# Attention maxima of a sparse-attention decoder step: edge masks as VectorE additions instead of bf16 matmuls, and a new table of durations in the kernel's planner

## The chip, the cores and the metric

The kernel runs on one core of a Trainium2 chip. Times are device microseconds of that core: the median of several runs, and, for everything that is read from a trace, one profiled execution. TensorE is called PE, VectorE DVE, ScalarE ACT, GpSimd POOL and SyncE SP, as in the profile.

## The reference, cut to what matters

One layer of a hybrid decoder: an adaptive norm, one input projection, native sparse attention beside a gated MLP, and an output projection, for a prompt of 1024 tokens and for 8 tokens that are decoded against caches. The change touches the prompt's attention, and there the maxima that keep the exponentials of two branches in range: `s` over the selected blocks, `w` over a sliding window of 512 keys.

```python
def block(i):
    start = i * Q_BLOCK
    qb = lax.dynamic_slice_in_dim(q, start, Q_BLOCK, axis=1)
    qpos = start + jnp.arange(Q_BLOCK, dtype=jnp.int32)
    kwb = lax.dynamic_slice_in_dim(kw_pad, start, band, axis=1)
    ...
s_s = jnp.einsum('bqgrd,bqgnld->bqgrnl', qg, k_sel).astype(jnp.float32) * scale
s_s = jnp.where(m_s, s_s, NEG).reshape(B, Tq, N_KV, GQA, n_sel * L_SLC)
p_s = jax.nn.softmax(s_s, axis=-1).reshape(B, Tq, N_KV, GQA, n_sel, L_SLC)
m_w = ((kwpos[None, :] <= qpos[:, None]) & (kwpos[None, :] > qpos[:, None] - WINDOW)
       & (kwpos[None, :] >= 0))[None, :, None, None, :]
s_w = jnp.einsum('bqgrd,bkgd->bqgrk', qg, kw).astype(jnp.float32) * scale
p_w = jax.nn.softmax(jnp.where(m_w, s_w, NEG), axis=-1)
```

## The kernel before, in words

The work runs in stages that overlap at their edges: loads, modulation and projections of the prompt (to about 260 us of the trace), the decoded tokens with their caches (to about 430 us), the prompt's attention (to about 807 us), the merge of the two mixers (to about 937 us) and the output projection. Large products are split into a high and a low fp32r half, so that three fp32r matmuls stand for one fp32 product.

Attention goes over 16 tiles, `TILES`: a key/value group `g` and a block `i` of 128 queries, four heads at a time. For each tile three streams of instructions are recorded:

- `front(g, i)` loads the queries, splits them into `R` and `R2`, computes the compressed branch (`kc`, `ce`, `pg`) and, by `peaks()` and `maxima()`, the row maxima of raw scores: `wm`, one for each 128 keys of the window, and `bm`, one for each 64-key block. From these, with the choice of blocks, it makes the biases `BT`, which PE transposes into `R2`.
- `scores()` computes 128 keys by 512 (four heads of 128 queries) into a bank of the tag `st`, two fp32r matmuls each; ACT takes the exponential `pt`, and POOL cuts the edge blocks with an affine select. `low()` splits `pt` into `p`'s high and low halves on ACT, DVE and POOL.
- `outputs()` multiplies `p` with the values `vv` into a bank `pv`, three matmuls for each of 132 groups; `weigh()` and `close()` apply sums and gates.

`maxima()` takes up to four 128-column blocks at a time: one matmul `mx<-L,R` for the adjacent blocks of a head, into one of two banks of the tag `mx`, then one DVE reduction. A block on the diagonal (`k == i`) needs a triangle mask, and the oldest of a window (`k == i - 4`) its complement, the far mask. They are added by PE, as a matmul of a bf16 identity with a bf16 mask, into the same bank. The two `mx` banks serve every transpose and small product of the stage too.

Beside attention PE works through gate pieces, `ct_proj` (24 fp32r matmuls of 344 columns, `mm<-hh,c0h` and the like), which depend on nothing in attention and are let in at a pace that `paced()` ties to the value groups done.

No order is written out by hand. While the program is recorded, the class `Plan` keeps an estimated time for each engine, tile and bank: `op()` looks up when operands are free, `cost()` gives a duration, and `go()` takes, among the streams that can go on, the one whose next operand is due first against PE's estimated time, and by rank after that. What `cost()` says thus decides in which order each engine's queue is written; on the chip each engine then follows its queue in order and waits where an operand is late. Every instruction is issued through one line of the class `Proxy`, L218 before the change and L235 after it, so rows are told apart by their tiles' names.

Of the kernel before, what the change touches and what calls it, by code (L numbers as in the profile page):

```python
# [28 lines left out]
class Pack:  # L29


    def __init__(self):
        self.cols, self.parts, self.n = {}, [], 0
# [57 lines left out]
MAIN, PACK1, PACKD, ROPE, EROWS = _tables()  # L91


class Plan:
# [6 lines left out]
    def __init__(self):  # L101
        self.free, self.bus, self.slots, self.rings, self.seen = {}, 0.0, {}, {}, {}
        self.columns, self.streams, self.last = {}, [], 0.0
        self.gone, self.since, self.spilled = 0.0, {}, {}

    def tile(self, pool, uid, shape, dtype, name, bufs=1):
        t = pool.tile(shape, dtype, name=name, tag=name, bufs=bufs)
        n = self.rings.get((uid, name), 0)
        self.rings[uid, name] = n + 1
        self.slots[t.tensor.name] = (uid, name, n % bufs)  # L110
        return t
# [54 lines left out]
    def cost(self, engine, name, outs, ins, size, start):  # L166
        if engine == "pe":
            n, m, dt = ins[1].free_size(), ins[0].free_size(), ins[0].dtype
            cost, passes = max(n / 2.4 + 2.5, (26 if dt == BF else 104) * m / 128), 1
            if name == "transpose":  # L170
                passes = 2
            elif dt == F32:
                cost, passes = max(4 * n / 2.4 / (4 if m <= 32 else 1), 208 * m / 128), 4
            tick = int(start // self.TICK)
            self.columns[tick] = self.columns.get(tick, 0.0) + passes * n * ins[0].partition_size() / 128
            return cost * (2 if self.cold(start) else 1)
        if engine == "dve":
            plain = name == "tensor_copy" and outs[0].space == ins[0].space
            return 67 + (0.52 if plain else 1.042) * size
        if engine == "act":  # L180
            return (280 if len(ins) > 1 else 70) + 0.834 * size
        if name == "affine_select":
            return 65 + 1.4 * size
        if name == "tensor_scalar":
            return max(330 + 0.83 * size, 3.61 * size - 28)
        return (300 + 165 * size if size < 16 else 70 + 2.27 * size)

    def op(self, engine, name, outs, ins):
        size = max(x.free_size() for x in outs + ins)
        start = self.free.get(engine, 0.0)  # L190
        for x in ins:
            start = max(start, self.after(x, True, engine))
        for x in outs:
            start = max(start, self.after(x, False, engine))
        for x in ins + outs:
            if x.space == PSUM:
                start = max([start] + [y[2] for y in self.seen.get(self.box(x)[0], ()) if y[3] != engine])
        if "dma" in name:
            self.free[engine] = start + (1038.0 if engine == "pool" else 450.0)
            self.bus = max(self.bus, self.free[engine]) + outs[0].free_nbytes() * outs[0].partition_size() / 359.0  # L200
            end = self.bus + 2000.0
        else:
            cost = self.cost(engine, name, outs, ins, size, start)
            self.free[engine] = start + cost
            end = start + cost + self.LATE[engine]
            self.last = max(self.last, end + 60.0)
        for x in ins:
            self.note(x, False, end, engine)
        for x in outs:
            self.note(x, True, end, engine)  # L210
# [50 lines left out]
def nsa_gmlp_step(ctx: ExitStack, tc: tile.TileContext, a: dict):  # L261
    nc = tc.nc
    plan = Plan()
    dve, act, pool, pe, sp = (plan.engine(e, n) for e, n in (
        (nc.vector, "dve"), (nc.scalar, "act"), (nc.gpsimd, "pool"), (nc.tensor, "pe"), (nc.sync, "sp")))
# [13 lines left out]
    def region(name, side):  # L279
        return Region(name, side)  # L280
# [4 lines left out]
    def bank(tag):  # L285
        return plan.tile(psum, "psum", [128, 512], F32, tag, 2)
# [12 lines left out]
    turn = [0]  # L299
# [5 lines left out]
    def dma(out, in_):  # L305
        sp.dma_start(out, in_)

    def rows(name, n, m=128):

        return bass.AP(tensor=a[name].tensor, offset=a[name].offset, ap=[[0, m], [1, n]])  # L310

    def consts(pack, tile_, name, p=128):
        lo, hi = pack.cols[name]
        return tile_[:p, lo:hi]


    const = region("const", "left")
    main = const.tile([128, MAIN.n], F32, name="main")

    def K(name, p=128):  # L320
        return consts(MAIN, main, name, p)

    ident = K("ident")
    ident_bf = const.tile([128, 128], BF, name="ident_bf")
    tri_bf = const.tile([128, 128], BF, name="tri_bf")
    far_bf = const.tile([128, 128], BF, name="far_bf")
    minus_half = const.tile([128, 16], F32, name="minus_half")
    gates = const.tile([128, NT + 1, 24], F32, name="gates")
    wck = const.tile([128, 2, 128], F32, name="wck")
# [232 lines left out]
    pk = rawreg.tile([128, PACK1.n], F32, name="pk")  # L562
# [8 lines left out]
    def rope_tab(which):  # L571

        c = top.tile([128, NT + 1, 2, 64], F32, name="rt")
        g = gq[:, which, None, :]
        for hf in range(2):
            lo, other = slice(hf * 32, hf * 32 + 32), slice(32 - hf * 32, 64 - hf * 32)
            n = [128, NT + 1, 32]
            pool.tensor_tensor(c[:, :, 0, lo], rope[:, :, 0, :], g[:, :, lo].to_broadcast(n), op=OP.mult)
            pool.tensor_tensor(c[:, :, 1, lo], rope[:, :, 1 + hf, :], g[:, :, other].to_broadcast(n), op=OP.mult)
        return c  # L580

    def constants():

        dma(rope, a["rope"])
        dma(gq.rearrange("p a b -> p (a b)"), rows("qk_g", 128))
        pool.memset(wck, 0.0)
        for j in range(2):
            for g in range(2):
                dma(wck[g * 64:g * 64 + 64, j, g * 64:g * 64 + 64], a["w_cmp"][j])
        yield lambda: stage[0] >= 3  # L590
        tabs["k"] = rope_tab(1)
        yield lambda: stage[0] >= 6
        dve.tensor_copy(ident_bf, ident)
        yield 0
        dve.tensor_copy(tri_bf, consts(PACK1, pk, "tri"))
        dve.tensor_copy(far_bf, consts(PACK1, pk, "far"))
        yield lambda: all(("k", i) in passed for i in ORDER)
        tabs["q"] = rope_tab(0)
        dma(pd, a["packd"])
        dma(pg_i, a["pages"])  # L600
        yield pg_i
        dve.tensor_copy(pg_f, pg_i)
        dve.tensor_scalar(idx, pg_f, 16.0, consts(PACKD, pd, "jmod"), op0=OP.mult, op1=OP.add)
# [905 lines left out]
    built, part = set(), set()  # L1509
# [63 lines left out]
    def front(g, i):  # L1573

        nb = 2 * (i + 1)
        j = TILES.index((g, i))
# [11 lines left out]
        b = bank("mx").rearrange("p (r q) -> p r q", r=4)  # L1588
# [12 lines left out]
        def maxima(w, flat, c, width, dst):  # L1601

            b = bank("mx")
            part = flat[c:c + 4]
            j = 0
            while j < len(part):
                r, k = part[j]
                n = sum(1 for x in part[j:] if x[0] == r)
                pe.matmul(b[:, j * 128:(j + n) * 128], lhsT=R[:, r, :], rhs=L1[g, w][:, k * 128:(k + n) * 128],
                          start=True, stop=False, skip_group_check=True)  # L1610
                for x in range(n):
                    mask = tri_bf if k + x == i else far_bf if w and k + x == i - 4 else None
                    if mask is not None:
                        pe.matmul(b[:, (j + x) * 128:(j + x + 1) * 128], lhsT=ident_bf, rhs=mask,
                                  start=False, stop=False, skip_group_check=True)
                j += n
            n = len(part) * 128
            dve.tensor_reduce(dst[:, c * 128 // width:(c * 128 + n) // width],
                              b[:, :n].rearrange("p (a x) -> p a x", x=width), op=OP.max, axis=AX.X)
# [16 lines left out]
        b = bank("mx")[:, :256].rearrange("p (r c) -> p r c", r=4)  # L1636
# [13 lines left out]
        if i == 0:  # L1650
# [5 lines left out]
                           op=OP.mult)  # L1656
# [14 lines left out]
        b = bank("mx")  # L1671
# [19 lines left out]
        b = bank("mx")  # L1691
# [326 lines left out]
```

## Time and profile before

| what | value |
|---|---|
| median of 3 runs | 1044.58 us (1043.27 to 1046.47) |
| the profiled execution, its own time | 1043.74 us |
| its span, first to last instruction | 1041.8 us |
| mean granted TensorE clock | 0.995 |
| PE busy | 1015.5 us, 5763 matmuls |
| DVE busy | 632.8 us |
| ACT busy | 448.4 us |
| POOL busy | 305.2 us |

Matmuls are pipelined, and a matmul's shown duration overlaps the next one's. What one costs is seen from the distance between starts. The same holds, less strongly, for DVE.

### The profile page before, as it was taken

How to read it: one execution, taken by the hardware profiler on the slowest of the kernel's cores; microseconds unless marked ns; L12 is line 12 of the kernel's file. 1: busy time of each engine (PE TensorE's matmuls, PEld its weight loads, DVE VectorE, ACT ScalarE, POOL GpSimd, SP SyncE). 2: the span in 40 equal slices, each digit the busy share in tenths (PEclk: the TensorE clock that was granted, in tenths of full speed). 3: DMA queues.
4: the chain of work that ended last, by engine and by line, in shares of the span. 5: the costliest groups of instructions: out<-in, count | busy, mean ns of one | idle time of the engine just before them, and what ended most of it. 6: DMA issues, size and time to landing. Idle time of an engine off the chain costs nothing.

```text
span 1041.8 us, 16312 instructions
## 1 busy us (share of the span) xinstructions
PE 1015.5 (97%) x5763; PEld 878.7 (84%) x5763; DVE 632.8 (61%) x1340; ACT 448.4 (43%) x951; POOL 305.2 (29%) x332
## 2 busy tenths in 40 slices
PE   6899999999999999999999999999999999999998
PEld 2489887879999999987787787788788999998776
DVE  1673686454668766568679868885753247574322
ACT  2762122001322254766776676676666242232000
POOL 0442475454321110013444332433333100251000
PEclk8999999999999999999999999999999999999999
DMA  8836441104775745422121121111111478654321
GB/s 294 292 95 211 155 131 51 61 21 152 271 213 162 245 154 184 141 68 60 51 56 56 47 68 50 45 51 57 50 57 58 138 238 259 182 161 137 129 90 64
DMA packets 106312, 130.35 MB, mean 125 GB/s; under 512 B 27299, under 2 KB 71525, under 8 KB 106230
## 3 DMA queue, kind: packets, MB, share of 16 engines
q1 hardware_dynamic: 101622, 112.53, 34.4%
q0 software_dynamic: 4608, 16.78, 5.2%
q8 instruction: 45, 0.74, 0.3%
q14 instruction: 37, 0.30, 0.1%
HBM read 98.96 MB, written 30.23 MB: 124 GB/s over the span
## 4 chain that ended last, share of the span: by engine, by line
PE 81%; DVE 7%; ACT 4%; DMA 3%; issue 2%; POOL 1%; SPq 1%; DVEq 0%; ACTq 0%; POOLq 0%
PE mm L218 33%; PE pv L218 20%; PE st L218 15%; PE mx L218 14%; DVE p L218 2%; DMA graw<-in_w_ada_dram 1%; DVE ce L218 1%; DVE bm L218 1%; ACT p L218 1%; ACT pt L218 1%; DVE wm L218 1%; SPq L218 1%; DVE c0l L218 0%; DVE hl L218 0%; POOL m L218 0%
## 5 line engine op out<-in xcount | busy, mean ns | idle before, releaser
L218 PE MATMUL pv<-p,vv 128*128 128x512 f32 (+1 forms) x396 | 112.2, 402 | 0.1
L218 PE MATMUL mm<-hh,c0h 128*128 128x344 f32 x320 | 105.1, 328 | 0.0
L218 PE MATMUL mm<-hh,c1h 128*128 128x344 f32 x320 | 104.9, 328 | 0.0
L218 ACT ACTIVATE pt<-st 128x512 f32<-128x512 f32 x132 | 78.6, 595 | 55.7 <-PE st L218 53.7
L218 PE MATMUL mm<-hl,c0h 128*128 128x344 f32 x320 | 102.2, 319 | 0.0
L218 PE MATMUL mm<-hh,c1l 128*128 128x344 f32 x320 | 102.2, 319 | 0.0
L218 PE MATMUL mm<-hh,c0l 128*128 128x344 f32 x320 | 102.1, 319 | 0.0
L218 PE MATMUL mm<-hl,c1h 128*128 128x344 f32 x320 | 102.1, 319 | 0.0
L218 PE MATMUL st<-R,L 128*128 128x512 f32 (+1 forms) x264 | 88.8, 418 | 0.0
L218 PEld LDWEIGHTS pv<-p,vv 128*128 128x128 f32 (+1 forms) x396 | 65.8, 173 | 21.9 <-DVE p L218 1.4
L218 DVE TENSOR_TENSOR p<-pt,p 128x512 fp32r<-128x512 f32 x88 | 70.3, 807 | 13.0 <-ACT p L218 12.5
L218 POOL TENSOR_TENSOR p<-pt,p 128x512 fp32r<-128x512 f32 x44 | 59.1, 1344 | 43.9 <-ACT p L218 43.9
L218 ACT ACTIVATE p<-pt 128x512 fp32r<-128x512 f32 x94 | 59.1, 629 | 16.6 <-POOL pt L218 14.4
L218 PE MATMUL mx<-L,R 128*128 128x512 f32 (+3 forms) x204 | 63.1, 362 | 1.2 <-DVE bm L218 0.6
L218 PEld LDWEIGHTS mm<-hh,c0h 128*128 128x128 f32 x320 | 60.4, 189 | 2.8 <-issue 0.2
L218 POOL TENSOR_SCALAR_AFFINE_SELECT pt<-pt 128x512 f32<-128x512 f32 x40 | 27.8, 696 | 119.0 <-ACT pt L218 117.1
L218 PEld LDWEIGHTS mm<-hh,c1h 128*128 128x128 f32 x320 | 60.3, 188 | 2.4 <-issue 0.2
L218 PEld LDWEIGHTS mm<-hh,c0l 128*128 128x128 f32 x320 | 60.2, 188 | 2.2
L218 PEld LDWEIGHTS mm<-hh,c1l 128*128 128x128 f32 x320 | 60.2, 188 | 2.2
L218 PEld LDWEIGHTS mm<-hl,c1h 128*128 128x128 f32 x320 | 60.1, 188 | 0.0
L218 PEld LDWEIGHTS mm<-hl,c0h 128*128 128x128 f32 x320 | 60.1, 188 | 0.0
L218 ACT ACTIVATE th<-mm 128x344 f32<-128x344 f32 x68 | 30.9, 454 | 58.3 <-PE mm L218 58.0
(495 smaller groups left out, 2622.1 us busy)
## 6 DMA issues: line engine op xcount, KB each, us to landing
t_db<-th SPq DMA_DIRECT2D x24, 172.0 KB
t_da<-th SPq DMA_DIRECT2D x24, 172.0 KB
th<-t_db SPq DMA_DIRECT2D x24, 172.0 KB
th<-t_da SPq DMA_DIRECT2D x24, 172.0 KB
graw<-in_w_ada_dram SPq DMA_DIRECT2D x16, 256.0 KB
araw<-in_w_ada_dram SPq DMA_DIRECT2D x16, 256.0 KB
xt<-in_x_dram SPq DMA_DIRECT2D x8, 512.0 KB
eraw<-in_w_ada_dram SPq DMA_DIRECT2D x16, 256.0 KB
```

The costliest lines, as they stand in the source:

```text
L218: r = getattr(real, name)(*args, **kw)
```

## The change

Two parts. In `maxima()` the mask matmuls go, and after the score matmuls of a bank DVE adds the fp32 mask in place in PSUM, one instruction for all blocks of the bank that need the same mask; the masks are kept in fp32 and the bf16 identity goes. In `Plan`, `cost()` and `op()` get other numbers: fp32r matmuls cost 0.4375 ns a column and 7 ns instead of 1/2.4 and 2.5; a price (`turn`) is put on changes between three kinds of matmul (split fp32r, full arrays in fp32, bf16 or transposes, and partial fp32); reciprocals and ACT instructions from SBUF or on few partitions cost more; and transfers take longer, above all those in rows under 512 bytes.

```diff
+            form, passes, turn = "split", 1, 0.0
+            if dt == FR and name != "transpose":
+                cost = max(0.4375 * n + 7.0, 104 * m / 128)
+                turn = {"split": 0.0, "full": 85.0, "part": 190.0}[self.form]
...
-            self.bus = max(self.bus, self.free[engine]) + outs[0].free_nbytes() * outs[0].partition_size() / 359.0
-            end = self.bus + 2000.0
+            self.bus = max(self.bus, self.free[engine]) + outs[0].free_nbytes() * outs[0].partition_size() / (179.5 if short else 359.0)
+            end = self.bus + (4200.0 if short else 2200.0)
...
-    ident_bf = const.tile([128, 128], BF, name="ident_bf")
-    tri_bf = const.tile([128, 128], BF, name="tri_bf")
-    far_bf = const.tile([128, 128], BF, name="far_bf")
+    tri = const.tile([128, 128], F32, name="tri")
+    far = const.tile([128, 128], F32, name="far")
...
-                for x in range(n):
-                    mask = tri_bf if k + x == i else far_bf if w and k + x == i - 4 else None
-                    if mask is not None:
-                        pe.matmul(b[:, (j + x) * 128:(j + x + 1) * 128], lhsT=ident_bf, rhs=mask,
-                                  start=False, stop=False, skip_group_check=True)
                 j += n
+            for mask, edge in ((tri, i), (far, i - 4 if w else -1)):
+                at = [j for j, (_, k) in enumerate(part) if k == edge]
+                if at:
+                    step = at[1] - at[0] if len(at) > 1 else 1
+                    x = b.rearrange("p (a x) -> p a x", x=128)[:, at[0]:at[-1] + 1:step, :]
+                    dve.tensor_tensor(x, x, mask[:, None, :].to_broadcast([128, len(at), 128]), op=OP.add)
```

What the two parts do to the order is seen at three places. The first is PE's queue amid the maxima of one tile (`R_5931` before and `R_5928` after belong to it; `L_4323` and `L_4261` are its keys, `vv` the values, `mm` a gate piece). Before:

```order
L218 MATMUL mx<-L_4323,R 128x512
L218 LDWEIGHTS ident_bf
L218 MATMUL mx<-tri_bf,ident_bf 128x128
L218 MATMUL mx<-L_4323,R 128x512
L218 MATMUL st<-R,L_4324 128x512
L218 MATMUL st<-R_5931,L_4327 128x512
L218 MATMUL pv<-p_6391,vv_4330 128x512
```

After, from the same matmul of the maxima on:

```order
L235 MATMUL mx<-L_4261,R 128x512
L235 MATMUL mx<-main,s_6388 128x128 x4
L235 MATMUL st<-R,L_4262 128x512
L235 MATMUL st<-R_5928,L_4265 128x512
L235 MATMUL pv<-p_6485,vv_4268 128x512
L235 MATMUL pv<-p_6485,vv_4268 64x512
L235 MATMUL pv<-p_6485,vv_4268 128x512
L235 MATMUL mm<-hh,c0h 128x344
```

The identity's load and the mask are gone from PE, the next maxima come later, and a gate piece stands between them.

The second is DVE's queue at that place (`bm` and `wm` are the maxima, `p` the split of the probabilities). Before:

```order
L218 TENSOR_TENSOR p_6366<-pt,p_6366 128x512
L218 TENSOR_REDUCE wm<-mx 128x4
L218 CAST p_6421<-pt 128x512
L218 TENSOR_REDUCE bm<-mx 128x8
L218 TENSOR_TENSOR p_6421<-pt,p_6421 128x512
L218 TENSOR_REDUCE bm<-mx 128x8 x2
```

After:

```order
L235 TENSOR_TENSOR mx<-mx,tri 128x128
L235 TENSOR_REDUCE bm<-mx 128x8
L235 TENSOR_TENSOR p_6511<-pt,p_6511 128x512
L235 TENSOR_REDUCE bm<-mx 128x8
L235 TENSOR_TENSOR mx<-mx,tri 128x128
L235 TENSOR_REDUCE bm<-mx 128x8 x2
L235 CAST p_6571<-pt 128x512
```

Each reduction of a bank with an edge block now has an addition ahead of it, in the queue from which PE also gets the low halves `p`.

The third is PE's queue near the start (`graw` and `araw` are slices of the modulation's weights, `mrow` its result that is turned, `xt` the first tokens that are transposed). Before:

```order
L218 MATMUL mx<-pk,pe_122 128x1 x2
L218 MATMUL mx<-main,xt 128x128 x8
L218 MATMUL mm<-graw,cs 32x512
L218 MATMUL mm<-araw,cs 32x512
L218 MATMUL mm<-graw,cs 32x512
```

After:

```order
L235 MATMUL mx<-pk,pe_121 128x1 x2
L235 MATMUL mm<-graw,cs 32x512
L235 MATMUL mm<-araw,cs 32x512
L235 MATMUL mm<-graw,cs 32x512
L235 MATMUL mm<-araw,cs 32x512
L235 MATMUL mx<-main,xt 128x128 x8
```

The first transposes of x moved behind four matmuls of the second part of the modulation.

## Rows read from the trace of the kernel before

**Rows 1.** The page: span, busy time by engine, and the chain that ended last.

```profile
span 1041.8 us, 16312 instructions
PE 1015.5 (97%) x5763; PEld 878.7 (84%) x5763; DVE 632.8 (61%) x1340; ACT 448.4 (43%) x951; POOL 305.2 (29%) x332
PE 81%; DVE 7%; ACT 4%; DMA 3%; issue 2%; POOL 1%; SPq 1%; DVEq 0%; ACTq 0%; POOLq 0%
```

**Rows 2.** Windows by stage: length, busy time by engine (instructions), granted clock, transfers.

```profile
0.00:52.00 52.00, 39.75 (x185) 20.23 (x186) 21.48 (x53) 24.53 (x48) 14.04 (x27) 0.93 0.86 293
52.00:430.00 378.00, 375.56 (x2221) 341.38 (x2221) 235.06 (x498) 117.86 (x267) 132.69 (x134) 1.00 0.47 151
430.00:469.00 39.00, 38.88 (x248) 34.57 (x246) 25.28 (x62) 25.83 (x62) 4.29 (x7) 1.00 0.29 82
469.00:781.00 312.00, 305.62 (x1716) 251.77 (x1716) 235.96 (x526) 213.51 (x457) 114.66 (x125) 0.99 0.19 54
781.00:989.00 208.00, 207.61 (x1194) 193.31 (x1193) 100.60 (x185) 66.11 (x119) 39.51 (x41) 1.00 0.53 163
989.00:1042.00 53.00, 48.06 (x208) 37.43 (x206) 14.40 (x21) 0.59 (x1) 0.00 (x0) 1.00 0.24 75
```

**Rows 3.** Groups by form on PE: the mask matmuls, count, busy and mean time.

```profile
L218 PE MATMUL mx<-tri_bf,ident_bf 128*128 128x128 bf16 x128 | 28.9, 230 | 0.0
L218 PE MATMUL mx<-far_bf,ident_bf 128*128 128x128 bf16 x32 | 7.4, 230 | 0.0
```

**Rows 4.** Timeline of PE around one mask: start, length, instruction.

```profile
574.65 0.86 PE L218 MATMUL pv<-p,vv 128*128 128x512 f32 x3
575.35 0.40 PE L218 MATMUL mx<-L,R 128*128 128x512 f32 x1
575.59 0.23 PE L218 MATMUL mx<-tri_bf,ident_bf 128*128 128x128 bf16 x1
575.63 0.47 PE L218 MATMUL mx<-L,R 128*128 128x512 f32 x1
575.94 0.62 PE L218 MATMUL st<-R,L 128*128 128x512 f32 x2
```

**Rows 5.** Groups by form on DVE, 469 to 790 us, that read PSUM.

```profile
L218 DVE TENSOR_REDUCE bm<-mx 128x8 f32<-128x512 f32 x66 | 44.2, 683 | 4.9 <-PE mx L218 4.4
...
L218 DVE TENSOR_TENSOR u<-mx,u 128x256 f32<-128x256 f32 x13 | 5.5, 424 | 8.5 <-PE mx L218 5.5 <-POOL u L218 1.6 <-POOL pt L218 1.3
...
L218 DVE TENSOR_TENSOR ce<-mx,main 128x128 f32<-128x128 f32 x13 | 3.8, 289 | 15.7 <-PE mx L218 15.7
```

**Rows 6.** Timeline of DVE: three operations in a row.

```profile
600.25 0.29 DVE L218 TENSOR_REDUCE cst<-ce 128x4 f32<-128x128 f32 x1
600.57 0.29 DVE L218 TENSOR_TENSOR ce<-ce,cst 128x128 f32<-128x128 f32 x1
600.78 0.68 DVE L218 TENSOR_REDUCE bm<-mx 128x8 f32<-128x512 f32 x1
```

**Rows 7.** The tile mx, 469 to 790 us: count, shortest, median and longest, first and last start.

```profile
L218 PE MATMUL mx<-tri_bf,ident_bf x106: 229/230/233, 469.0 to 761.2; 128*128 128x128 bf16 x106
...
L218 PE MATMUL mx<-far_bf,ident_bf x32: 229/230/233, 472.2 to 745.0; 128*128 128x128 bf16 x32
```

**Rows 8.** Windows, columns as in rows 2, of two fuller stretches of attention.

```profile
558.00:588.80 30.80, 29.51 (x162) 22.97 (x161) 27.67 (x64) 20.19 (x44) 13.81 (x16) 1.00 0.16 46
...
621.10:651.70 30.60, 30.45 (x168) 23.92 (x166) 27.30 (x66) 21.22 (x48) 7.41 (x9) 1.00 0.16 48
```

**Rows 9.** Timeline of PE near the start; in brackets the idle time before.

```profile
16.35 1.94 PE L218 MATMUL mx<-main,xt 128*128 128x128 f32 x8 [1.85 <-DVE xt L218]
```

**Rows 10.** Timeline of PE at the longest idle time of attention.

```profile
509.94 0.45 PE L218 MATMUL mx<-main,BT 128*128 128x128 f32 x1 [2.49 <-DVE BT L218]
```

**Rows 11.** Windows, columns as in rows 2, at and behind that idle time.

```profile
507.00:511.00 4.00, 1.51 (x5) 0.84 (x5) 3.93 (x9) 1.19 (x4) 2.50 (x3) 0.84 0.28 82
511.00:515.00 4.00, 4.00 (x19) 3.16 (x18) 0.17 (x2) 3.17 (x7) 1.20 (x1) 0.73 0.23 65
```

More of the change, by code (lines that the diff above doesn't have):

```diff
@@ L104, in __init__ @@
         self.gone, self.since, self.spilled = 0.0, {}, {}
+        self.form = "split"
     def tile(self, pool, uid, shape, dtype, name, bufs=1):
@@ L168, in cost @@
             n, m, dt = ins[1].free_size(), ins[0].free_size(), ins[0].dtype
[L169 to L173, printed above, removed]
+            form, passes, turn = "split", 1, 0.0
+            if dt == FR and name != "transpose":
+                cost = max(0.4375 * n + 7.0, 104 * m / 128)
+                turn = {"split": 0.0, "full": 85.0, "part": 190.0}[self.form]
+            elif name == "transpose" or dt == BF:
+                form, passes = "full", 2 if name == "transpose" else 1
+                cost = max(0.4375 * n + 7.0, (26 if dt == BF else 104) * m / 128)
+                turn = 190.0 if self.form == "part" else 0.0
+            elif m <= 64 and n > 128:
+                form, passes, cost = "part", 4, 0.4375 * n * 4 * m / 128 + 3
+                turn = 0.0 if self.form == "part" else 140.0
+            else:
+                form, passes, cost = "full", 4, max(4 * (0.4375 * n + 7.0), 208 * m / 128)
+                turn = 190.0 if self.form == "part" else 0.0
+            self.form = form
             tick = int(start // self.TICK)
             self.columns[tick] = self.columns.get(tick, 0.0) + passes * n * ins[0].partition_size() / 128
-            return cost * (2 if self.cold(start) else 1)
+            return cost * (2 if self.cold(start) else 1) + turn
         if engine == "dve":
             plain = name == "tensor_copy" and outs[0].space == ins[0].space
+            if name == "reciprocal":
+                return 80 + 18 * size
             return 67 + (0.52 if plain else 1.042) * size
         if engine == "act":
-            return (280 if len(ins) > 1 else 70) + 0.834 * size
+            if len(ins) > 1:
+                return 280 + 0.834 * size
+            p, space = outs[0].partition_size(), (ins or outs)[0].space
+            return (70 if space == PSUM else 94) + 0.834 * size + (105 if p < 128 and (p != 64 or size == 256) else 0)
         if name == "affine_select":
@@ L198, in op @@
         if "dma" in name:
-            self.free[engine] = start + (1038.0 if engine == "pool" else 450.0)
-            self.bus = max(self.bus, self.free[engine]) + outs[0].free_nbytes() * outs[0].partition_size() / 359.0
-            end = self.bus + 2000.0
+            self.free[engine] = start + (1038.0 if engine == "pool" else 500.0)
+            short = min(4 * x.ap[-1][1] for x in outs + ins[:1]) < 512
+            self.bus = max(self.bus, self.free[engine]) + outs[0].free_nbytes() * outs[0].partition_size() / (179.5 if short else 359.0)
+            end = self.bus + (4200.0 if short else 2200.0)
         else:
@@ L592, in constants @@
         yield lambda: stage[0] >= 6
-        dve.tensor_copy(ident_bf, ident)
         yield 0
-        dve.tensor_copy(tri_bf, consts(PACK1, pk, "tri"))
-        dve.tensor_copy(far_bf, consts(PACK1, pk, "far"))
+        dve.tensor_copy(tri, consts(PACK1, pk, "tri"))
+        dve.tensor_copy(far, consts(PACK1, pk, "far"))
         yield lambda: all(("k", i) in passed for i in ORDER)
```

## The prediction

> **What bounds the kernel now.** I read the page's busy shares first, then the stages, then the waits inside one stage. TensorE (PE) is busy for 1015.5 of 1041.8 us and carries 81% of the chain that ended last; VectorE (DVE) carries 7% of it [rows 1]. So a microsecond of PE work is worth about a microsecond, unless another engine takes PE's place. The stages [rows 2] show where PE is not full: 12.25 us are idle in the first 52 us, 4.94 us at the end, 2.44 us over 52 to 430, and 6.38 us in the attention stage, 469 to 781. Nothing is left to win outside those places. In the attention stage DVE is already busy for 235.96 of 312 us, a share of 0.76, and that is the engine to which the change gives work.
>
> **The masks leave PE.** The program has 128 triangle masks and 32 far masks as bf16 matmuls [rows 3]. Their shown 230 ns is not what they cost, since matmuls overlap; the price is read from starts. In [rows 4] a mask starts at 575.59 and the next matmul at 575.63, so the mask itself holds PE for 0.04 us. That next matmul, of 512 columns in fp32r, gives way only after 0.31 us (575.63 to 575.94), where three that follow their own kind take 0.70 us (574.65 to 575.35), 0.233 each. The return from a bf16 matmul to the fp32r kind costs the difference, 0.08 us. In PE's order fp32r matmuls that stand behind one of another kind fall from 290 to 133, so 157 returns go. The sum is 160 x 0.04 + 157 x 0.08 = 6.4 + 12.6 = 19.0 us. It lies wholly on the engine that sets the end; PE rows on either side of a mask show no idle time. The 160 weight loads of the identity overlap the matmuls and are not counted again.
>
> The Trainium skill (TensorE: Matmul & The Clock Gate, Back-to-back issue gap) prices a lone 128-column matmul at 134 cycles of 2.4 GHz; by that alone 160 masks would be worth an estimated 8.9 us, and the time would be 1035.7 us, inside the forecast's own range. The rows differ on both sides of that figure, since the mask is shorter there and the matmul behind it longer, and the rows decide.
>
> **The masks arrive on DVE.** There they become 136 additions in place in PSUM: 120 of 128 columns, 12 of 256, 4 of 512. No such operation is in the trace. The nearest rows [rows 5] are an addition of a PSUM tile and an SBUF constant, 128 columns, 289 ns; one of 256 columns, 424 ns; and a read of 512 columns of PSUM, 683 ns. That gives 120 x 0.289 + 12 x 0.424 + 4 x 0.683 = 34.7 + 5.1 + 2.7 = 42.5 us. The bounds come from starts [rows 6]: an operation whose successor needs its result holds DVE for 0.32 us (600.25 to 600.57), one whose successor does not for 0.21 us (600.57 to 600.78). All 120 small ones at the one or the other, and the rest scaled alike, make 47 or 31 us. I take 42.5, because the maximum behind a mask always needs its result, while of two masks in one bank the first need not hold up the second. The maximum's bank, one of only two, is held longer by the same 0.3 us per mask. The copies of the two masks at the start replace casts of 0.22 us and weigh nothing.
>
> The Trainium skill (VectorE: DVE Perf Modes, Rules for kernel authors) speaks against the change: it advises to keep the number of chained DVE operations small, since each pays for the emptying of its pipeline whether or not the next depends on it. The 0.32 us pair agrees and the 0.21 us pair does not; by the rule alone the masks cost the upper 47 us, and the sum below would be an estimated 4 us worse.
>
> **What DVE gives back.** In the attention stage lie 106 of the triangle and all 32 far matmuls [rows 7], so 86 + 32 = 118 of the 136 additions by the same proportion, or 37 us of the 42.5. DVE would need 236 + 37 = 273 us there. PE would need 312 - 138 x 0.119 = 295.6 us (0.119 is 19.0/160). DVE at 273 of 295.6 is a share of 0.92. The fullest stretches of some 30 us that the trace shows are at 27.67/30.80 = 0.90 and 27.30/30.60 = 0.89, with PE still idle for only 1.3 and 0.15 us [rows 8]. So I let DVE set the stage at a share of 0.90: 273/0.90 = 303.3 us, a gain of 8.7 us and not 16.4. The other 22 matmuls lie ahead of 469 us, where [rows 2] leave DVE room, and give 22 x 0.119 = 2.6 us. Behind a late mask stand, on DVE's queue, the low halves of the probabilities and the maxima; for them wait PE's value matmuls and the transposed biases.
>
> **The table.** It changes the order everywhere, not the work: each engine issues the same instructions apart from the masks. Where gate pieces (24 fp32r matmuls each) fill PE, the order has 73 of them before the last value matmul, as before, but 61 instead of 57 by the 72nd of 132 value groups, and 69 instead of 70 by the 120th. That puts filler where DVE is full and I count it as what lets DVE reach 0.90. At the start the first 61 transfers on SP's queue stand as before, and PE takes four of the next eight quarter matmuls ahead of the first transposes of x, for which it now waits 1.85 us [rows 9]; the gain is between nothing and that, the loss up to as much again if the first projection then waits for x. I take nothing. Over 52 to 430 and after 781 there is under 3 us of idle time [rows 2], so a better order can hardly win there; a worse one is given the same 3 us.
>
> **The sum.** 1043.74 us of the profiled execution (span 1041.8 and 1.9 around it) - 8.7 - 2.6 = 1032.4. The median of the three runs is 0.84 us above that execution, which makes 1033.3; I say 1033.
>
> **The rivals.**
> A full gain: PE stays the bound, because DVE can go above 0.90 when its work is planned with the longer durations, or because the masks cost nearer 31 us (then DVE needs 236 + 27 = 263 us, under 295.6 even at 0.90). The time is 1044.6 - 19.0 = 1025.6, and 1021.4 if the one costly wait below also goes. For it: DVE has 76 us without work. Against it: it must lose nearly all of them.
>
> Slower: DVE comes late for the transposed biases (BT), PE stops and its clock falls. This happens once in the trace. The transpose of BT waits 2.49 us for DVE, until 509.94 [rows 10]; in the next stretches the granted clock averages 0.84 and 0.73 [rows 11], between the 2.4 GHz level and the 1.2 GHz one, which loses 4.00 x 0.16 + 4.00 x 0.27 = 1.7 us of full clock. One such event costs 4.2 us. The Trainium skill (TensorE: Matmul & The Clock Gate, Why this matters for your kernels) tells to avoid idle gaps between bursts of matmuls because the clock drops behind them; the trace agrees at this one place. With 16 tiles and a BT each, five more events use up the 19.0 us, and eight make 1044.6 - 19.0 + 33.6 = 1059. Put as a share, DVE must keep above 273/314.6 = 0.87 in the stage (314.6 is 312 and the 2.6 us won ahead of it); at 0.85 the stage takes 321 us and the time is 1051. For it: the stage's mean is 0.76 today, and additions lengthen exactly the chain that ends in BT. Against it: the stretches at 0.90 saw no such stop.
>
> No change: the masks win what is forecast, and the new order loses it, above all before 430 us, where 12 us are idle and x, the modulation and the weights arrive in a close race. The time is 1041 to 1048. Against it stands that the first transfers keep their order.
>
> **How the numbers follow.** The forecast has 0.55 (1027 to 1040), the full gain 0.23 (1018 to 1027), no change 0.10, slower 0.12. The time is that of the forecast. The range reaches from 1020 to 1044: it takes in the full gain nearly to its end and most of the no-change case, and leaves out the slower one and a little below. What a measurement can tell from no change is about 0.3%, 3.1 us. Faster by more than that, under 1041.4, is the forecast, the full gain and a small part of no change: 0.80. The same is most of no change, 0.08; slower 0.12.
>
> **What the profile after would show.** Right: no bf16 matmuls; DVE busy near 675 us; 136 additions in PSUM at 0.2 to 0.33 us from start to start for 128 columns; PE busy some 19 us less; PE's waits in the attention stage grown from about 6 to about 14 us, with DVE named. The price of a mask on PE is wrong if PE's busy time falls by only 9 us; the cap is wrong if DVE's share there is above 0.92 without waits, or under 0.87 with BT waits and half-clock stretches; the silent part is wrong if the first 52 us differ by more than 2 us.

## The result, and the profile after

The changed kernel takes 1063.11 us (median of 4 runs, 1061.17 to 1065.21) against 1045.28 us of the kernel before beside it: a ratio of 1.0173 [1.0147, 1.0199], so slower by 1.7%, with the whole interval above 1. The forecast was 1033. The profiled execution took 1061.17 us, with a mean granted clock of 0.996 (0.995 before).

The page after, as [rows 1]: span, busy time, and the chain that ended last.

```profile
span 1059.5 us, 16225 instructions
PE 1010.0 (95%) x5603; PEld 871.2 (82%) x5603; DVE 672.0 (63%) x1475; ACT 448.3 (42%) x951; POOL 306.1 (29%) x332
PE 31%; DVE 14%; ACT 3%; issue 3%; POOL 2%; DMA 1%; SPq 0%; POOLq 0%; ACTq 0%; DVEq 0%
```

160 matmuls are gone, DVE has 39.2 us more work, and PE's share of the chain that could be followed fell from 81% to 31% (the shares add up to 54% of the span, so this row says little). The span grew by 17.7 us: PE's idle time went from 1041.8 - 1015.5 = 26.3 to 1059.5 - 1010.0 = 49.5 us, 23.2 more, while its busy time fell by 5.5.

Windows by stage after, as [rows 2]:

```profile
0.00:52.00 52.00, 40.44 (x179) 21.43 (x180) 20.87 (x51) 25.53 (x49) 14.36 (x27) 0.93 0.87 296
52.00:430.00 378.00, 368.86 (x2155) 330.15 (x2154) 229.81 (x491) 112.42 (x255) 132.18 (x134) 1.00 0.46 147
...
469.00:781.00 312.00, 291.23 (x1556) 240.55 (x1557) 263.54 (x633) 207.54 (x443) 108.20 (x119) 1.00 0.18 54
781.00:989.00 208.00, 205.13 (x1194) 191.06 (x1194) 111.11 (x205) 77.41 (x145) 47.30 (x49) 1.00 0.51 159
```

PE is now idle for 20.77 us of the attention stage (6.38 before) and for 9.14 us between 52 and 430 us (2.44 before), a stretch in which no mask stands (the first starts at 430.5 us before). What PE waits for in and around attention, 430 to 830 us, was of before and is now (engine, tile, its releaser: us, times, longest):

```profile
PE mx L218 <- DVE BT L218: 3.1, 2, 2.5
PE mx L218 <- DVE bm L218: 0.9, 2, 0.6
PE mx L218 <- DVE wm L218: 0.7, 2, 0.5
```

```profile
PE mx L235 <- DVE wm L235: 5.7, 10, 1.3
PE mx L235 <- DVE bm L235: 5.4, 12, 1.2
PE mx L235 <- DVE BT L235: 5.2, 6, 1.9
```

The one long stop for BT became 28 short ones, most of them for a bank of the maxima. The attention stage's clock is now 1.00 (0.99 before): none of the 17.7 us comes from a slower clock there.

### The profile page after: what moved, and what is told of

It reads as the page before. It is cut to its first block, busy times and chain, and to the rows that moved or that the text cites. A ratio compares the mean times of both kernels' runs of the same rounds, so it can differ in the third digit from the quotient of the medians.

```text
span 1059.5 us, 16225 instructions
## 1 busy us (share of the span) xinstructions
PE 1010.0 (95%) x5603; PEld 871.2 (82%) x5603; DVE 672.0 (63%) x1475; ACT 448.3 (42%) x951; POOL 306.1 (29%) x332
## 4 chain that ended last, share of the span: by engine, by line
PE 31%; DVE 14%; ACT 3%; issue 3%; POOL 2%; DMA 1%; SPq 0%; POOLq 0%; ACTq 0%; DVEq 0%
PE mm L235 11%; PE pv L235 7%; PE mx L235 6%; PE st L235 6%; DVE p L235 4%; DVE bm L235 2%; DVE wm L235 2%; DVE mx L235 2%; DVE BT L235 1%; DVE imp L235 1%; ACT pt L235 1%; POOL m L235 1%; ACT u L235 0%; DMA th<-t_da 0%; POOL u L235 0%
## 5 line engine op out<-in xcount | busy, mean ns | idle before, releaser
L235 PE MATMUL mm<-hh,c0l 128*128 128x344 f32 x328 | 105.0, 320 | 2.2 <-DVE c0l L235 2.2
L235 PE MATMUL mm<-hl,c0h 128*128 128x344 f32 x328 | 104.7, 319 | 0.0
L235 PE MATMUL st<-R,L 128*128 128x512 f32 (+1 forms) x264 | 85.7, 406 | 0.0
L235 ACT ACTIVATE p<-pt 128x512 fp32r<-128x512 f32 x94 | 59.0, 629 | 15.3 <-POOL pt L235 13.5
L235 PE MATMUL mx<-L,R 128*128 128x512 f32 (+3 forms) x204 | 54.4, 340 | 7.2 <-DVE bm L235 2.6
```

Of the source, the lines that this page charges most:

```text
L235: r = getattr(real, name)(*args, **kw)
```

## The experiments

Each was timed beside the kernel before on the same chip (its medians there lie between 1044.18 and 1045.47 us), and the ratio is to that. "Idle" is PE's idle time (length less busy time) in windows at the same times as above; stages move by some us from kernel to kernel. "Left" is the number of gate pieces, counted in the trace (24 matmuls each, 84 in all), that start behind the last value matmul of attention; PE uses them there as filler for the merge of the two mixers.

| kernel | us | ratio | idle 52-430 | idle 469-781 | idle 781-989 | left |
|---|---|---|---|---|---|---|
| before | 1044.58 | | 2.4 | 6.4 | 0.4 | 10.8 |
| after | 1063.11 | 1.0173 [1.0147, 1.0199] | 9.1 | 20.8 | 2.9 | 10.8 |
| e1_masks_only | 1049.92 | 1.0054 [1.0036, 1.0072] | 2.3 | 13.7 | 4.2 | 7.8 |
| e2_table_only | 1068.65 | 1.0250 [1.0209, 1.0292] | 9.7 | 12.1 | 1.0 | 18.8 |
| e3_no_masks_old_table | 1031.26 | 0.9880 [0.9860, 0.9900] | 2.4 | 8.2 | 0.5 | 10.2 |
| e4_no_masks_new_table | 1049.72 | 1.0057 [1.0035, 1.0079] | 11.5 | 9.7 | 2.3 | 10.8 |
| e5_pe_durations | 1079.68 | 1.0333 [1.0310, 1.0357] | 12.1 | 17.0 | 0.4 | 24.5 |
| e6_act_dve_durations | 1048.45 | 1.0030 [1.0019, 1.0041] | 3.3 | 3.2 | 8.2 | 6.0 |
| e7_transfer_durations | 1050.88 | 1.0054 [1.0040, 1.0068] | 3.4 | 5.4 | 5.7 | 8.2 |
| e8_margin_in_attention | 1074.33 | 1.0274 [1.0243, 1.0304] | 11.2 | 12.2 | 20.0 | 6.0 |
| e9_extra_additions | 1059.54 | 1.0130 [1.0113, 1.0146] | 2.1 | 9.4 | 7.4 | 6.8 |
| e10_no_masks_act_durations | 1041.80 | 0.9958 [0.9941, 0.9974] | 2.5 | 2.6 | 12.6 | 6.0 |
| e11_no_masks_reserve | 1041.20 | 0.9960 [0.9946, 0.9975] | 2.9 | 9.4 | 3.1 | 10.0 |
| e12_no_masks_margin | 1051.17 | 1.0054 [1.0038, 1.0071] | 2.9 | 5.7 | 15.4 | 6.0 |
| e13_pe_base_only | 1059.33 | 1.0139 [1.0115, 1.0163] | 8.0 | 10.1 | 0.3 | 19.0 |
| e14_pe_turns_only | 1058.38 | 1.0138 [1.0112, 1.0165] | 5.3 | 8.4 | 0.9 | 16.8 |
| e15_no_masks_short_pe | 1071.40 | 1.0262 [1.0241, 1.0283] | 6.2 | 13.6 | 17.7 | 6.0 |
| e16_change_without_pe_part | 1077.29 | 1.0310 [1.0286, 1.0335] | 3.5 | 17.2 | 19.7 | 6.0 |
| e17_before_half_per_cent | 1041.93 | 0.9977 [0.9964, 0.9990] | 2.4 | 4.7 | 1.0 | 12.8 |
| e18_after_half_per_cent | 1063.23 | 1.0195 [1.0178, 1.0212] | 10.0 | 17.7 | 3.6 | 10.8 |

### Masks and table apart

Each half alone, and both tables without any mask.

> The additions on VectorE with the old table: the first part of the change alone, same result. Theory A (VectorE comes late: the additions hold the two mx banks and stand ahead of the biases in VectorE's queue, whatever the table): PE waits as in the changed kernel, so 1055 to 1065 us, with PE's waits for bm, wm and BT over 12 us in attention. Theory B (the table's new order is what costs; the additions alone are worth the sum): 1027 to 1036 us.

> The new table with the masks still on PE as bf16 matmuls: the second part alone, same result. Theory A: near the kernel before or a little slower, 1043 to 1053 us, with some 7 us of the loss between 52 and 430 us, which the masks can't touch. Theory B: the table costs 20 us and more, 1060 to 1075 us.

> No mask on any engine (the maxima then take in keys that the masks would cut; the exponentials' own masks stay), old table: what leaving PE is worth where VectorE gets nothing. Both theories: if 0.119 us for a mask on PE is right, 1024 to 1028 us; if the shorter PE queue only uncovers waits for other engines, over 1032 us.

> No mask on any engine, new table. Theory A: the additions cost what the changed kernel lost, so 1028 to 1037 us here, some 28 us under it. Theory B: the new order's loss stays, 1045 us or more.

e1 has the additions with `cost()` and `op()` as before, e2 the mask matmuls with `cost()` and `op()` as after. e3 (old table) and e4 (new table) leave these lines out and put nothing in their place:

```diff
-                for x in range(n):
-                    mask = tri_bf if k + x == i else far_bf if w and k + x == i - 4 else None
-                    if mask is not None:
-                        pe.matmul(b[:, (j + x) * 128:(j + x + 1) * 128], lhsT=ident_bf, rhs=mask,
```

The medians as a table of the two parts:

| masks | old table | new table | table costs |
|---|---|---|---|
| matmuls on PE | 1044.68 | 1068.65 | +24.0 |
| additions on DVE | 1049.92 | 1063.11 | +13.2 |
| none | 1031.26 | 1049.72 | +18.5 |

The 1063.11 comes from another set of runs than the rest, beside 1045.28. e2 and e4 came out as Theory B had it; e1 and e3 lie between the ranges of their two alternatives. Each half loses by itself, and the two are not independent. With the old table the masks' leaving PE is worth 13.4 us and the additions cost 18.7, so that the move loses 5.2; with the new table they are worth 18.9 and cost 13.4, so that the move wins 5.5 (1068.65 to 1063.11). The table loses in every row. At 1031.26 us e3 beats both kernels. Without masks the maxima also run over keys that POOL's select cuts later, so what the softmax subtracts is larger or equal; it cancels in the quotient, as long as it isn't so far above the allowed scores that their exponentials vanish. That bound is what e3 gives up.

Span, mean granted clock and busy time of e3, then of e1, which issue the same 5603 matmuls:

```profile
core 0: 1028.7 us, clock 0.996
PE 999.4 (97%) x5603; PEld 873.9 (85%) x5603; DVE 633.0 (62%) x1340; ACT 448.6 (44%) x951; POOL 305.9 (30%) x332
```

```profile
core 0: 1048.1 us, clock 0.988
PE 1009.2 (96%) x5603; PEld 879.0 (84%) x5603; DVE 679.3 (65%) x1475; ACT 450.6 (43%) x951; POOL 302.8 (29%) x332
```

With the masks gone PE is busy for 16.1 us less than before. With the additions the same matmuls are shown as 9.8 us busier. In e1 most of that is the clock: 0.012 of 1048.1 us against 0.004 of 1028.7 are an estimated 8 us of full clock more that are lost. In the changed kernel the mean clock is 0.996, as in e3, and the same matmuls are still shown as 1010.0 - 999.4 = 10.6 us busier. There it is waits that do not show as idle time, because a matmul's shown length reaches beyond the point at which the next one can start. Timeline of PE after:

```profile
524.08 0.32 PE L235 MATMUL mm<-hh,c1h 128*128 128x344 f32 x1
524.24 0.32 PE L235 MATMUL mm<-hh,c1l 128*128 128x344 f32 x1
```

These start 0.16 us apart and are shown as 0.32 us long, so a wait of up to 0.16 us behind one of them leaves no idle time. Taken from start to start, less idle time and outside the stretches at half clock, the fp32r matmuls that follow their own kind take 8 us more in the changed kernel than in e3, while about as many stand behind another kind (148 and 150): a changed mix of kinds is not the reason. The account of the change is then 23.2 us more idle time and 10.6 us of longer shown lengths, most of them hidden waits, less 16.1 us of work, which are the 17.7 us of the span.

In e1 DVE is not at its limit where PE stops longest. The attention stage of e1 and windows of 10 us, columns as in [rows 2]:

```profile
469.00:781.00 312.00, 298.31 (x1599) 252.06 (x1598) 270.03 (x639) 211.26 (x449) 107.41 (x119) 0.98 0.18 53
440.00:450.00 10.00, 7.50 (x49) 7.07 (x48) 7.68 (x21) 5.94 (x15) 0.40 (x1) 0.98 0.38 114
450.00:460.00 10.00, 10.00 (x56) 9.41 (x55) 6.57 (x17) 5.06 (x13) 0.64 (x1) 0.85 0.23 65
500.00:510.00 10.00, 6.29 (x41) 5.57 (x39) 5.13 (x8) 6.55 (x15) 3.79 (x4) 1.00 0.30 84
510.00:520.00 10.00, 9.86 (x53) 9.21 (x54) 7.68 (x20) 7.40 (x18) 2.28 (x3) 0.83 0.26 72
540.00:550.00 10.00, 10.00 (x57) 8.59 (x56) 9.60 (x23) 7.43 (x19) 3.19 (x4) 1.00 0.14 39
550.00:560.00 10.00, 10.00 (x56) 8.69 (x56) 9.48 (x28) 7.36 (x15) 2.29 (x3) 1.00 0.22 61
560.00:570.00 10.00, 10.00 (x55) 8.73 (x55) 9.86 (x20) 7.58 (x15) 5.83 (x8) 1.00 0.33 97
...
590.00:600.00 10.00, 8.82 (x35) 6.61 (x34) 9.30 (x22) 4.45 (x10) 1.93 (x2) 0.83 0.11 28
...
720.00:730.00 10.00, 7.93 (x36) 6.35 (x35) 9.52 (x25) 3.03 (x6) 3.33 (x4) 0.83 0.34 98
```

From 540 to 570 us DVE is busy for 0.96 of the time and PE is shown as never idle. PE stops at 440 to 450 and 500 to 510 (2.50 us for `bm` and 3.34 for `ce`, the longest stops), where DVE is busy for 0.77 and 0.51, and over the 10 us behind each the granted clock averages 0.85 and 0.83, between the 2.4 and the 1.2 GHz level. From 590 to 600 and from 720 to 730 (here a stop of 2.03 us for `wm`) it averages 0.83 too, and there DVE is busy for 0.93 and 0.95. So a share of DVE's time alone does not tell where this stage stops. Nor is the share without meaning: in the changed kernel 12.9 of the 20.7 us that PE is idle between 470 and 780 lie in the 17 of 31 windows of 10 us in which DVE is busy for 0.88 or more, as in these two:

```profile
490.00:500.00 10.00, 8.21 (x38) 5.97 (x38) 9.79 (x18) 5.79 (x11) 4.68 (x6) 1.00 0.14 44
700.00:710.00 10.00, 8.44 (x42) 6.41 (x43) 9.59 (x25) 4.34 (x9) 2.11 (x3) 1.00 0.11 27
```

### Is it DVE's load, or the bank that is held?

An addition occupies DVE and keeps one of two banks longer. Here the masks stay on PE, and DVE makes as many additions (at most 256 columns) on an SBUF tile that nobody reads, right behind each maximum.

> The kernel before, masks on PE, plus as many additions of the same size on VectorE as the change has (those of four blocks cut to two), each behind the maximum of its bank and on a tile of SBUF that nobody reads: VectorE's work without the longer hold of the bank. Same result. Theory L (VectorE's load is what costs): 1055 to 1068 us. Theory H (a bank of mx is held longer, and PE stands at the next use of the two): 1044 to 1050 us.

```diff
+            for edge in (i, i - 4 if w else -1):
+                at = min(2, sum(1 for _, k in part if k == edge))
+                if at:
+                    x = extra[:, :at, :]
+                    dve.tensor_tensor(x, x, ident[:, None, :].to_broadcast([128, at, 128]), op=OP.add)
```

1059.54 us, 14 us over before, with 41.1 us more on DVE. Load on DVE's queue costs 14 us here, with no bank held and PE's work unchanged, where the additions cost 18.7. It isn't the load alone: the planner knows of these additions too and writes another order for them, and no run separates the two. Little of the loss is visible as idle time in attention (9.4 us); the attention stage uses 39.2 gate pieces in place of 35.2, and the merge behind it, with 6.8 left, is idle for 7.4.

### Which part of the table

On the kernel before, each part of the table alone:

> The kernel before with only the new PE durations in the table (and the price of turns); masks on PE, same result. Theory C (the longer PE durations let the planner hold operands for ready that are due just then, so that small delays reach PE): most of the table's loss of 24 us is here, 1058 to 1070 us. Theory D (the transfers' longer durations reorder loads and decode): 1042 to 1050 us here.

> The kernel before with only the new durations of ACT and of VectorE's reciprocal; masks on PE, same result. Theories C and D alike: within 5 us of the kernel before, 1040 to 1050 us, since longer durations there put more work between a producer and PE.

> The kernel before with only the new durations of transfers; masks on PE, same result. Theory C: 1041 to 1048 us. Theory D: 1055 to 1070 us, with PE's waits between 52 and 430 us grown by 10 us or more.

The cores of the three, in this order (PE's new lengths and the prices of a change of kind; reciprocals and ACT; transfers):

```diff
+                cost = max(0.4375 * n + 7.0, 104 * m / 128)
+                turn = {"split": 0.0, "full": 85.0, "part": 190.0}[self.form]
...
+            if name == "reciprocal":
+                return 80 + 18 * size
...
+            end = self.bus + (4200.0 if short else 2200.0)
```

PE's durations cost 34 us, more than Theory C allowed, the others 3 and 5; all three together cost 24. The transfers' part (e7) lies between the two theories' ranges, and its idle time between 52 and 430 us grew by 1 us and not by the 10 of Theory D. The parts don't add up: what one breaks, another mends in part. In e5 PE's idle time grows where no maxima are at work at all, 260 to 430 us (170.00 us busy of 170 before), and in attention:

```profile
260.00:430.00 170.00, 163.92 (x1083) 156.90 (x1084) 116.46 (x219) 70.05 (x160) 27.98 (x33) 1.00 0.64 203
469.00:781.00 312.00, 295.01 (x1587) 231.39 (x1586) 229.27 (x502) 214.49 (x451) 119.12 (x130) 1.00 0.16 48
```

DVE's share of attention is 0.73 here, below the 0.76 of before, and PE still waits 17 us. Only 59.5 pieces are used by the end of attention, against 73.2 before.

The two halves of PE's part, e13 with the new lengths (the first line) and `turn` left out of what `cost()` returns, e14 with the old lengths and the second line:

> The kernel before (masks on PE), of the new table only the length of PE's own instructions (0.4375 ns a column and 7 ns, for all kinds), without the prices of a change of kind. Theory E, that any longer estimate of PE's work makes the planner put fewer gate pieces between a producer on DVE or ACT and PE, so that its real waits reach PE: 1055 to 1075 us, fewer than 33 of the 84 pieces inside the attention stage (35 before, 25 with the whole PE part). Rival, that the prices of the changes of kind are what misleads: 1043 to 1048 us and 35 pieces or more.

> The kernel before (masks on PE), of the new table only the prices of a change of kind on PE (85, 140 and 190 ns), with the old lengths. Theory E: the changes are some hundred in the attention stage, fewer than the instructions that the lengths touch, so a smaller loss than with the lengths, 1047 to 1062 us. Rival, that the prices of a change are what misleads: 1065 us or more, near the 1079.68 of the whole PE part.

```diff
+                cost = max(0.4375 * n + 7.0, 104 * m / 128)
...
+                turn = {"split": 0.0, "full": 85.0, "part": 190.0}[self.form]
```

They cost 15 and 14 us, and both move pieces from attention (30.5 in place of 35.2) to behind it. The prices of a change of kind are no smaller a cause than the lengths, other than theory E had it; added up, the two make 29 of the 34 us.

### Mending the order

If pieces stand too late, a margin that takes operands for late sooner should bring them forward. On the changed kernel:

> The changed kernel, but in the attention stage the planner takes a stream only where its operand is due 0.3 us ahead of PE, instead of up to 0.1 us behind. Same result. Theory C: PE's waits in attention fall by 10 us and more, 1045 to 1055 us. If VectorE is simply too busy there with the additions, a margin can't help: 1059 to 1067 us.

```diff
-    plan.go(until=lambda: 1 in closed)
+    plan.go(until=lambda: 1 in closed, slack=300.0)
```

Idle time in attention falls from 20.8 to 12.2 us, nearly the 10 us that were meant, and 20.0 us turn up behind it: the filler is used up, and the time lies above both ranges. Waits of e8's PE, and the merge's window:

```profile
PE st L235 <- ACT xh L235: 15.4, 4, 6.5
```

```profile
833.00:937.00 104.00, 88.64 (x529) 86.69 (x529) 47.16 (x91) 27.09 (x52) 10.70 (x11) 0.88 0.59 178
```

PE waits for `xh`, the high half of what the merge multiplies, with nothing left to do meanwhile, and the granted clock averages 0.88 there. The same was tried three ways on the kernel without masks:

> No masks on any engine, and of the new table only the durations of ACT and of the reciprocal. With those alone PE waited 7 us less in attention and 10 us more behind it, so here 1028 to 1036 us if that exchange stays, under 1028 us if the shorter queue changes it.

> As the run with no masks and ACT's durations, but the pace keeps 10 gate pieces and not 6 for the time behind attention. If the pieces left at the end of attention cover the first loads of the merge, PE's wait there goes without a new one: 1020 to 1028 us. If the pieces are missed more in attention: over 1030 us.

> No masks, old table, and in attention the planner takes a stream whose operand is due just when PE is free, instead of up to 0.1 us after. If PE's waits in attention are operands that come a little late, 1025 to 1031 us; if the pieces run out for it, 1031 to 1040 us.

e10 is e6 without masks, e11 is e10 with four more pieces kept back (the first pair of lines), e12 is e3 with another margin in attention (the second pair).

```diff
-    SPANS, PACE_LEAD, PACE_FRONT, PACE_REST = 132, 12, 14, 6
+    SPANS, PACE_LEAD, PACE_FRONT, PACE_REST = 132, 12, 14, 10
...
-    plan.go(until=lambda: 1 in closed)
+    plan.go(until=lambda: 1 in closed, slack=0.0)
```

e10 and e12 use up the pieces (6 left) and wait 9.6 and 9.0 us for `xh`; e11 keeps 10, and the waits come back in attention (9.4 us of idle time). e10 and e12 lie above both of their ranges, e11 is the case of pieces missed in attention, and none comes near e3's 1031.26.

### Direction, and the change without PE's part

> The edge masks are left out of the maxima altogether, with the old table, and the length of PE's fp32r, bf16 and transposing instructions in the plan is cut by a tenth (0.9/2.4 ns a column and 2.5 ns). Theory E turned round: a shorter estimate of PE puts more gate pieces between producer and PE, so more than 36 pieces inside attention and less waiting there than the 20.5 us of the run without masks; under 1031 us if the pieces still reach for the stage behind attention, 1032 to 1045 if they run out there. Rival, that the estimate's length does not steer the pieces: within 2 us of 1031.26 and 35 to 36 pieces.

> The changed kernel (masks as additions on DVE) with the durations of PE put back as they were before; the new durations of ACT, of the reciprocals and of the transfers stay. If the PE part is what the table costs: 1045 to 1056 us, near the 1049.92 of the additions with the old table. If the other durations cost as much by themselves beside the additions: over 1060 us, near the 1063.11 of the whole change.

e15 has no masks and the line below; e16 is the changed kernel with `cost()` for PE as before.

```diff
-            cost, passes = max(n / 2.4 + 2.5, (26 if dt == BF else 104) * m / 128), 1
+            cost, passes = max(0.9 * n / 2.4 + 2.5, (26 if dt == BF else 104) * m / 128), 1
```

Neither came out near what was expected: e15 lies above both of its ranges, and e16 is over 1060 us, as its second case had it, but 14 us beyond the 1063.11 that went with it. A PE planned a tenth faster does bring pieces forward (78 used by the end of attention, 73.8 in e3), but it loses 40 us: the filler is gone behind attention, and waits in attention grow too. And without PE's part the change is slower by 14 us than with it, with 6 pieces left. Around the merge of e16:

```profile
840.00:860.00 20.00, 20.00 (x116) 19.90 (x116) 2.69 (x7) 4.21 (x9) 4.32 (x6) 0.88 0.17 49
860.00:880.00 20.00, 9.58 (x48) 7.92 (x46) 5.24 (x11) 6.01 (x13) 0.00 (x0) 0.72 0.73 229
880.00:900.00 20.00, 17.85 (x103) 17.64 (x103) 11.85 (x25) 4.98 (x11) 0.00 (x0) 0.85 0.71 210
900.00:920.00 20.00, 20.00 (x129) 20.00 (x128) 13.51 (x28) 5.63 (x11) 0.00 (x0) 1.00 0.83 256
```

PE is idle for 12.57 us between 860 and 900, all other engines have room, and from 840 to 900 the granted clock averages 0.72 to 0.88, between the two levels. So PE's durations are not bad in themselves. Longer ones put filler later, longer ones of the other engines (or shorter ones of PE) put it earlier, and either way some stretch is left without.

### Is any new order worse?

Then the order of before might only be a lucky one that every change of numbers leaves. A change of 0.4% in one number says nothing about durations, but it rewrites the order: in a line comparison of PE's matmuls in the traces 1,466 lines differ from before (e17) and 1,888 from after (e18). Between e13 and before it is 2,452, between e6 and before 1,568.

> The kernel before with one number of the planner moved by 0.4%: PE's fp32r, bf16 and transposing instructions are planned at 1/2.39 ns a column in place of 1/2.4. No real duration can be judged by that, but thousands of lines of PE's queue change places. Theory S, that the order before stands at a place that nearly any change of the numbers leaves for a worse one, whatever its direction or size: 1050 to 1065 us. Rival, theory D, that the direction and size of the numbers set the loss: 1042 to 1048 us.

> The changed kernel with the same small move: 0.4393 ns a column in place of 0.4375 in PE's fp32r, bf16 and transposing instructions. Theory S: the order after is one of many such orders and no choice one, so it moves by 5 us or more to either side of 1063.11, between 1050 and 1077. Theory D: 1060 to 1066 us.

The first pair of lines is e17, on the kernel before, the second e18, on the changed kernel, where the other line with this length has the same edit.

```diff
-            cost, passes = max(n / 2.4 + 2.5, (26 if dt == BF else 104) * m / 128), 1
+            cost, passes = max(n / 2.39 + 2.5, (26 if dt == BF else 104) * m / 128), 1
...
-                cost = max(0.4375 * n + 7.0, 104 * m / 128)
+                cost = max(0.4393 * n + 7.0, 104 * m / 128)
```

1041.93 and 1063.23: the first a little faster than before, the second the same as after. Theory S falls for rewritings of this extent: two new orders cost nothing. That the loss follows the size of a change in the numbers is not shown by that; the whole table, which changes most, costs less (24 us) than PE's part of it (34).

## Why the prediction was wrong

The forecast was 1044.6 - 11.3 for the masks and 0 for the table. Alone, the masks' part measured +5.2 (e1) and the table, put on top of it, +13.2 (after against e1); with the table first it is +24.0 and then -5.5 for the masks. The two misses, 16.5 and 13.2 us, are the 29.8 between 1033.3 and 1063.1.

- **The price of a mask on PE** was sized about right. Without masks PE's busy time falls by 16.1 us and the run by 13.4 (18.9 under the new table); 19.0 was forecast. The 155 returns to fp32r that are gone give back 13.5 us by starts (305 to 150 returns), where 157 for 12.6 us were forecast. PE's busy time in the changed kernel, which fell by only 5.5 us, was named as the sign that this price is wrong; it is no such sign, because waits hide in shown lengths.
- **The work on DVE** was right in busy time: 672.0 us, 675 forecast. From start to start each of the 120 small additions takes 0.32 to 0.34 us, so that they come to the prediction's upper 47 us and not to 42.5, and the first of two masks in one bank does hold up the second. Timeline of DVE after:

```profile
561.53 0.29 DVE L235 TENSOR_TENSOR mx<-mx,tri 128x128 f32<-128x128 f32 x1
561.85 0.30 DVE L235 TENSOR_TENSOR mx<-mx,far 128x128 f32<-128x128 f32 x1
562.19 0.69 DVE L235 TENSOR_REDUCE wm<-mx 128x4 f32<-128x512 f32 x1
```

- **"So I let DVE set the stage at a share of 0.90"** is the first step that failed. It gave 7.7 of the 19.0 us back; the additions took 18.7 (old table), an estimated 8 of them by the clock. PE's idle time in the stage was to grow to 14 us and grew to 20.8. The price is not a share alone: in e1 DVE goes to 0.96 with PE shown as full, and PE stops longest where DVE is at 0.51 and 0.77, since a bank or an operand is late there and no filler stands ahead of it in PE's queue. [rows 8] showed what cover can hide at those places, not what the stage can hide everywhere. e9 says that work on DVE that holds no bank, with the order planned for it, costs 14 us; whether the rest comes from the held bank wasn't separated.
- **"It changes the order everywhere, not the work ... a worse one is given the same 3 us"** is the second. Little idle time before bounds what a new order can win, not what it can lose. Between 52 and 430 us, where at most 3 us were allowed, idle time grew by 6.7. The pieces were compared at three points only and read as a help for DVE that the table gives; the places without one were not looked for. The help is not the table's: by the 72nd value group 57.75 pieces have started before and 61.25 after, but 62.5 in e1 (additions, old table) and 53.75 in e2 (the table alone). That the table loses is shown three times (+24.0, +13.2, +18.5), and e17 and e18 show two rewritten orders that don't.
- **The start** was right: 40.44 us busy in the first 52 against 39.75, and the wait for `xt` is gone.
- **The rivals.** "Slower" gave 1051 for a share of 0.85, and the share is 263.54/312 = 0.845. e1 shows its mechanism, stops with a lower clock behind them at four places, for `bm`, `ce` and `wm` rather than BT. That its 1051 is near e1's 1049.92 is luck in part: e1's share is 270.03/312 = 0.865, for which the same working gives 1046. In the changed kernel the stops are short and the clock stays at 1.00, and the table does the rest. "No change" laid a loss of about the masks' 11 us on the new order; the order did cost 13.2, but the masks' gain that it was to eat up wasn't there.

What stays open: why these numbers lead to just these places. That pieces stand late under longer PE durations and early under the others is counted in the runs that change one part, but no count of them forecasts a time: with 10.8 left there are kernels of 1044.58, 1049.72 and 1063.11 us. e4 and the changed kernel lose much ahead of attention, where 35.2 pieces stand in place of 38.

## What to carry to other kernels

An order made by a planner is a part of the kernel's work: when its durations change, look for the places where filler no longer stands between a producer and the engine that sets the end, and bound the loss by the latencies that the filler hides, not by the idle time that is left. Work that moves from the bounding engine to one with room costs what it delays in that engine's queue; take the free share of the second engine for no cover. And before work is moved, ask whether it is needed: here leaving the masks out won 13.4 us, where moving them lost 5.2 (old table), at the price of the bound named above. What such a move is worth depends on the order around it: under the new table the same move won 5.5.

## What the runs showed of the hardware

The same 5603 matmuls were shown as busy for 999.4 us in one order (e3) and for 1010.0 in another (the changed kernel), both at a mean granted clock of 0.996: a 344-column matmul is shown as 0.32 us where the next can start 0.16 us behind it, so short waits stand in shown lengths, and busy time counts them as work. In the kernel before a bf16 mask held PE for 0.04 us from start to start (median of 160), and the fp32r matmul of 512 columns behind one for 0.31 to 0.34 us, against 0.233 behind its own kind. The granted clock did not follow the longest single stop: behind stops of 2.50 and 3.34 us in e1 it was 0.85 and 0.83 over 10 us, and it was 0.83 again at 590 to 600, where the longest wait was 0.65 us and PE was idle for 1.18 of 10, and at 720 to 730, with a stop of 2.03; behind a stop of 1.89 us in the changed kernel (for BT, until 523.21) it stayed at full speed, as all over 469 to 781 (1.00).
